# A gate/up kernel stage whose scale sums move along TensorE's products and whose operand buffers change hands product by product

## The chip, the cores and the metric

The kernel runs on one core of a Trainium2 chip. A core has five engines with an instruction stream each: TensorE (PE, with PEld for its weight loads), VectorE (DVE), ScalarE (ACT), GpSimd (POOL) and SyncE (SP), which here issues all DMA transfers. Each engine takes its instructions in the order in which the program has them, and semaphores make it wait for others. The metric is the time of one execution in microseconds (us). Before the change the median of three runs is 2845.04 us (2842.7 to 2848.43).

## The reference, cut to what matters

One layer of an encoder over 2048 tokens of width 1024. The change touches the channel mixer:

```python
h2 = rmsnorm(r, norm2_g[i])
gate = dwconv(h2 @ ffn_wg[i], ffn_conv_w[i], FFN_CONV_LEFT) + ffn_conv_b[i]
r = r + (jax.nn.gelu(gate) * (h2 @ ffn_wu[i])) @ ffn_wd[i]
```

`ffn_wg` and `ffn_wu` are 1024 x 2816, `ffn_wd` 2816 x 1024, the convolution has 3 taps along the tokens. Ahead of it stand the mixers and their output projection, behind it a gated per-layer embedding and a last norm.

## The kernel before, in words

**Arithmetic.** Every float32 operand is split into two float16 parts, high and low, scaled by a power of two, and a product is three float16 products of these parts. On top of it, a product of 2 x 2 blocks is made with seven block products instead of eight (Strassen's scheme in Winograd's form): `PROD` says which of the seven left and which of the seven right operands the products 1 to 7 take, `LEFT` and `RIGHT` say how the operands arise from the four blocks by sums and differences.

**Tiling of the gate/up stage.** The weights come in 22 groups n of 256 output columns, even n for the gate, odd n for the up projection; j = n // 2 counts pairs. The 2048 tokens are two halves u. A unit (n, u) is seven products of 12 matmuls 128x128 by 128x512 (line 1684). `units` (line 1687) puts the products of neighbouring units in turn: product 1 of a unit, then 3 and 7 of the unit before, then 2 and 5, then 4 of the unit before, then 6. So unit (n, 1)'s last product, 4, stands between products 5 and 6 of unit (n+1, 0). A product leaves its result in a bank of PSUM. Its evacuation goes over ACT (line 1859, products 1, 6, 5, 4) or over DVE as an addition (line 1864, products 2, 3, 7).

**Weight groups.** `pair_weights` prepares group n: two loads of 512 KB into two staging buffers (line 1789), the norm's gain on POOL (line 1792), the squares on ACT (line 1795), an add of the two sums on DVE (line 1797), and on PE a matmul with a matrix of ones that sums over the partitions, the scale matmul (line 1800), here called the sum. Six small DVE steps make the power of two from it (lines 382 to 392, `pow2_scale`). Then `operands` makes seven left operands: some need a POOL sum or difference of blocks first (line 1665), each is then split on ACT (line 1640) and DVE (line 1642) into its buffer. The buffers are two sets of seven, for even and odd n. The staging buffers are loaded again when all seven splits of a group are done. Before the change, the splits of group n begin when the last product of unit (n-2, 1) has been put into the program (`pdone`).

**Around it on the same engines.** For each pair j, `gate_tile` does the convolution and gelu of two gate tiles (lines 1906, 1909, 1911, 1913, 1917), `mult` multiplies with the up projection on POOL (line 1927), `act_post` splits the results and writes them out (lines 1945 to 1960), and `row_squares` loads rows of the down weights for their squares (lines 2026, 2028). Behind the stage, the down weights are loaded (line 2064) and split, the embedding's products run (line 438), two further sums stand on PE (line 567 for the embedding's weights, line 2049 for the down weights), and the down products follow.

**What sets the order.** The program is written by a list scheduler, `Sched`. Work is a set of generator streams; each yields a step with the engines and the nanoseconds that it is taken to last (`st`), an event to wait for (`W`) or memory to allocate (`M`). The scheduler keeps a planned time of each engine, and always issues the step with the earliest planned start (`LOOK` weighs a stream's priority against it). `lag` in a step adds to its planned start. An event carries the planned time at which it was fired. All this happens when the program is built; on the chip only the order of each engine's stream and the semaphores are left.

Of the kernel before, what the change touches and what calls it, by code (L numbers as in the profile page):

```python
# [16 lines left out]
S = SEQ = 2048  # L17
# [4 lines left out]
KB = 1024  # L22
# [4 lines left out]
SPOT, LX, LD = 0, 0, 0  # L27
ORDER = "q1 k1 lx1 lg1 lx3 v3 q0 k0 v0 q3 lx0 k3 lg3 k2 lg0 q2 v2 v1 z0 lx2 lg2 z1 z2 ow0 z3 ow1".split()
# [20 lines left out]
class Arena:  # L49
# [9 lines left out]
    def take(self, nbytes, high=False):  # L59
        nbytes = (nbytes + 63) // 64 * 64  # L60
        free = self.lists[nbytes <= 512]

        for page in (PAGE, 64) if nbytes % PAGE == 0 else (64,):
            for o, n in reversed(free) if high else free:
                off = (o + n - nbytes) // page * page if high else -(-o // page) * page
                if o <= off and off + nbytes <= o + n:
                    free.remove((o, n))
                    free += [x for x in ((o, off - o), (off + nbytes, o + n - off - nbytes)) if x[1]]
                    free.sort()
                    return Buf(self, off, nbytes)  # L70
        return None
# [79 lines left out]
class Sched:  # L151
# [43 lines left out]
    def settle(self, s):  # L195
# [11 lines left out]
        if kind == "m":  # L207

            if any(o.spec and o.spec[0] == "m" and o.prio < s.prio and o is not s for o in self.streams):
                return False  # L210
            got = []
            for n in s.spec[1]:
                b = self.A.take(n, s.spec[2])
                if b is None:
                    for x in got:
                        x.free()
                    return False
                got.append(b)
            self.value = got
            return True  # L220
# [63 lines left out]
def W(*name):  # L284
    return ("w", name)
# [52 lines left out]
class Kern:  # L338
# [1330 lines left out]
    def product(self, U, p):  # L1669
# [6 lines left out]
        for i in range(0, m, PER):  # L1676
# [6 lines left out]
            for j, (l, r) in enumerate(part):  # L1683
                self.nc.tensor.matmul(out, l, r, start=(p in (1, 2, 5) and i + j == 0), stop=(p in (2, 3, 4) and i + j == m - 1), skip_group_check=True)  # L1684
        S.spawn(U.evac(p), PR["evac"])
# [84 lines left out]
    def pair_weights(self):  # L1770
# [3 lines left out]
        for n in range(22):  # L1774
# [10 lines left out]
            ops = w.ops = [(b.f16(4, 128), b.f16(4, 128, at=KB)) for b in sets[n % 2]]  # L1785
# [12 lines left out]
            b = yield st(pe=20, bank=1)  # L1798
# [4 lines left out]
            if n > 1:  # L1803
                yield W("pdone", n - 2)
            blocks = [v[i][:, z * 4 : z * 4 + 4] for i in range(2) for z in range(2)]
            put = lambda i, a, w=w: self.split(a, *w.ops[i], 512, w.s)
# [841 lines left out]
```

## Time and profile before

| | |
|---|---|
| median of three runs | 2845.04 us |
| the profiled execution | 2846.02 us, its span 2844.3 us |
| mean granted TensorE clock | 0.961 |
| busy: PE, DVE, ACT, POOL | 90%, 63%, 52%, 34% |
| gate/up stage from behind the sum of group 1 | 1313.3 to 2151.8 us, 838.5 us |
| from there to the down products | 151.2 us |

A row of the timeline gives the start from the span's start, the length, the engine, the line, the operation with the tiles that it writes and reads, shapes, and a count where neighbours are merged; in brackets stands how long the engine was idle before and what released it. `arena` is the one tile in SBUF from which all buffers are cut, `P` a bank of PSUM. Matmuls overlap: the next begins before the modelled end of the one before. [...]

### The profile page before, as it was taken

The page shows a single profiled execution, that of the slowest core. Times are in us where ns is not written, and L with a number is a line of the kernel's source. Part 1 is how long each engine was busy: PE and PEld are TensorE (multiplying, and loading weights), DVE is VectorE, ACT ScalarE, POOL GpSimd, SP SyncE. Part 2 cuts the span into 40 slices and gives each one's busy share as a digit, 9 for nine tenths or more (in the row PEclk, how much of TensorE's full clock was granted, in tenths as well). Part 3 has the DMA queues.
Part 4 walks back from the last instruction along what each step waited for, and adds up shares of the span by engine and source line. Part 5 has one row for each costly group of instructions (what it writes and reads, how often), then busy time and mean ns, then how long its engine had stood idle before and what let it go on. Part 6 is the DMA issues. An engine that isn't in the chain of part 4 may idle for free. (4 is left out here: it accounts for less than half of the span.)

```text
span 2844.3 us, 39697 instructions
## 1 busy us (share of the span) xinstructions
PE 2563.4 (90%) x13918; PEld 1289.5 (45%) x13918; DVE 1797.1 (63%) x3717; ACT 1477.3 (52%) x3042; POOL 977.1 (34%) x686
## 2 busy tenths in 40 slices
PE   5997998889889987976999999999997599999898
PEld 2553454466466653432444444444443244444343
DVE  7668877878784776565566666667768831211358
ACT  6676857764566764254556656666556610101323
POOL 1135335536410022234555656555545600000000
PEclk9998999999999998988999999999999899999999
DMA  9332241475454467396132333323335854556963
GB/s 246 76 96 67 82 123 53 119 208 171 115 160 145 132 214 255 86 212 147 52 93 88 96 108 106 104 87 101 104 97 175 251 182 146 168 168 218 284 176 145
DMA packets 478279, 402.31 MB, mean 141 GB/s; under 512 B 203648, under 2 KB 407296, under 8 KB 478080
## 3 DMA queue, kind: packets, MB, share of 16 engines
q1 hardware_dynamic: 478080, 399.78, 48.2%
q8 instruction: 110, 1.80, 0.3%
q14 instruction: 89, 0.73, 0.1%
HBM read 231.39 MB, written 130.55 MB: 127 GB/s over the span
## 5 line engine op out<-in xcount | busy, mean ns | idle before, releaser
L1684 PE MATMUL P<-arena 128*128 128x512 f16 x5313 | 1163.4, 382 | 2.3 <-DVE arena L2094 1.4
L438 PE MATMUL P<-arena 128*128 128x512 f16 x4032 | 966.8, 389 | 56.3 <-DMA arena<-catl 13.6
L1684 PEld LDWEIGHTS <-arena 128*128 128x128 f16 x5313 | 523.4, 99 | 633.3 <-issue 19.1
L438 PEld LDWEIGHTS <-arena 128*128 128x128 f16 x4032 | 397.8, 101 | 491.2 <-issue 61.4
L1642 DVE SCALAR_TENSOR_TENSOR arena<-arena 128x512 f16<-128x512 f32 (+2 forms) x340 | 416.0, 1257 | 196.3 <-ACT arena L1640 196.1
L1665 POOL TENSOR_TENSOR arena<-arena 128x512 f32<-128x512 f32 (+1 forms) x208 | 367.9, 1770 | 293.9 <-DVE arena L1642 197.7
L1640 ACT ACTIVATE arena<-arena 128x512 f16<-128x512 f32 (+2 forms) x340 | 267.7, 821 | 289.4 <-DMA actd<-arena 65.4
L1927 POOL TENSOR_TENSOR arena<-arena 128x512 f32<-128x512 f32 x88 | 146.4, 1683 | 153.7 <-ACT arena L1917 90.4
L2094 DVE SCALAR_TENSOR_TENSOR arena<-P,arena 128x512 f32<-128x512 f32 x63 | 46.1, 749 | 241.4 <-PE P L1684 221.2
L538 POOL TENSOR_TENSOR arena<-arena 128x1024 f32<-128x1024 f32 (+1 forms) x41 | 82.9, 2027 | 300.6 <-DMA arena<-in_w_in_dram 175.7
L1859 ACT ACTIVATE arena<-P 128x512 f32<-128x512 f32 x176 | 103.5, 588 | 95.4 <-PE P L1684 80.5
L1222 POOL TENSOR_TENSOR arena<-arena 128x512 f32<-128x512 f32 x64 | 119.1, 1876 | 76.0 <-DVE arena L1172 62.2
L699 DVE SCALAR_TENSOR_TENSOR arena<-P,arena 128x511 f32<-128x511 f32 (+1 forms) x192 | 141.8, 742 | 2.0
L2121 ACT ACTIVATE arena<-arena 128x1024 bf16<-128x1024 f32 x16 | 16.9, 1055 | 228.8 <-DVE arena L2094 174.0
L1864 DVE TENSOR_TENSOR arena<-P,arena 128x512 f32<-128x512 f32 x132 | 89.3, 684 | 72.2 <-PE P L1684 68.3
L1792 POOL TENSOR_TENSOR arena<-arena 128x1024 f32<-128x1024 f32 x44 | 92.3, 2107 | 110.4 <-DMA arena<-in_w_gu_dram 51.8
L1419 ACT ACTIVATE arena<-P,arena 128x128 f32<-128x128 f32 x128 | 46.8, 365 | 88.9 <-PE P L1413 69.3
L1424 PE MATMUL P<-arena 128*128 128x128 f32 x256 | 60.3, 318 | 19.5 <-ACT arena L1422 12.8
L862 PE MATMUL P<-arena 128*128 128x512 f32 x128 | 66.3, 634 | 11.7 <-DVE arena L699 5.2
L1430 DVE SCALAR_TENSOR_TENSOR arena<-arena,P 128x128 f32<-128x128 f32 x128 | 43.7, 343 | 52.4 <-PE P L1425 23.4
L1125 POOL TENSOR_TENSOR arena<-arena 128x512 f32<-128x512 f32 x32 | 39.3, 1227 | 108.3 <-DVE arena L1122 90.1
L1274 PE MATMUL P<-arena 32*32 32x32 f32 (+1 forms) x1792 | 63.3, 208 | 13.3 <-issue 6.8
(232 smaller groups left out, 3380.7 us busy)
## 6 DMA issues: line engine op xcount, KB each, us to landing
arena<-hd SPq DMA_DIRECT2D x160, 256.0 KB, 3.1
actd<-arena SPq DMA_DIRECT2D x77, 512.0 KB, 3.7
arena<-actd SPq DMA_DIRECT2D x49, 704.0 KB, 4.1
arena<-in_w_gu_dram SPq DMA_DIRECT2D x44, 512.0 KB, 4.3
arena<-in_x_dram SPq DMA_DIRECT2D x32, 512.0 KB, 6.4
at<-arena SPq DMA_DIRECT2D x64, 256.0 KB, 2.8
arena<-at SPq DMA_DIRECT2D x128, 128.0 KB, 3.0
rd<-arena SPq DMA_DIRECT2D x32, 512.0 KB, 5.2
```

What stands on the lines that cost most here:

```text
L438: self.nc.tensor.matmul(out, l, r, start=(i + j == 0), stop=(i + j == m - 1))
L538: nc.gpsimd.tensor_tensor(at(i), at(i), gain[:, ks[i], None].to_broadcast([128, m, n]), op=ALU.mult)
L699: nc.vector.scalar_tensor_tensor(a[:, lo:hi], P[:, lo - sh : hi - sh], tp[:, j : j + 1], a[:, lo:hi], op0=ALU.mult, op1=ALU.add)
L1222: nc.gpsimd.tensor_tensor(pv[:, i % 2], a(slice(2 * i, 2 * i + 2)), b(slice(2 * i, 2 * i + 2)), op=ALU.mult)
L1640: nc.scalar.activation(hi, x, AF.Copy, scale=scale)
L1642: nc.vector.scalar_tensor_tensor(lo, x, scale, hi, op0=ALU.mult, op1=ALU.subtract)
L1665: nc.gpsimd.tensor_tensor(v[at], v[p], v[q], op=ALU.add if plus else ALU.subtract)
L1684: self.nc.tensor.matmul(out, l, r, start=(p in (1, 2, 5) and i + j == 0), stop=(p in (2, 3, 4) and i + j == m - 1), skip_group_check=True)
L1792: nc.gpsimd.tensor_tensor(v[i], v[i], c["g2"][:, :, None].to_broadcast([128, KT, 128]), op=ALU.mult)
L1859: nc.scalar.activation(d, P, AF.Copy)
L1864: nc.vector.tensor_tensor(d, P, d, op=ALU.add)
L1927: nc.gpsimd.tensor_tensor(v, v, U.buf.f32(2, 2, 4, 128)[:, i, s], op=ALU.mult)
```

## The change

It has three parts. First, the sum of a group gets a planned lag, 5000 ns for the groups from 2 on and 3000 ns for groups 0 and 1. Second, the splits no longer wait for the last product of unit (n-2, 1): each product fires an event "last" when it has been put into the program, the buffers of a set are handed on so that the operand made first gets the buffer whose last product comes first, and each split waits for that product alone. Third, an allocation of several buffers that finds no room on page bounds is tried again without them.

```diff
+AFTER_SUM = 5000
...
-            got = []
-            for n in s.spec[1]:
-                b = self.A.take(n, s.spec[2])
...
+            for pages in (True, False):
+                got = []
+                for n in s.spec[1]:
+                    b = self.A.take(n, s.spec[2], pages)
...
+        S.fire(U.key, "last", p)
         S.spawn(U.evac(p), PR["evac"])
...
-            ops = w.ops = [(b.f16(4, 128), b.f16(4, 128, at=KB)) for b in sets[n % 2]]
+            if n > 1:
+
+                old = [PROD[p][0] for p in (1, 2, 5, 6, 3, 7, 4)]
+                new = [i for i, _, _ in LEFT]
+                frees = {i: next(p for p in PROD if PROD[p][0] == k) for i, k in zip(new, old)}
+                sets[n % 2] = [sets[n % 2][old[new.index(i)]] for i in range(7)]
+            w.ops = [(b.f16(4, 128), b.f16(4, 128, at=KB)) for b in sets[n % 2]]
...
-            b = yield st(pe=20, bank=1)
+            b = yield st(pe=20, bank=1, lag=AFTER_SUM if n > 1 else 3000)
...
-            if n > 1:
-                yield W("pdone", n - 2)
...
-            put = lambda i, a, w=w: self.split(a, *w.ops[i], 512, w.s)
+
+            def put(i, a, n=n, w=w):
+                if n > 1:
+                    yield W(("gu", n - 2, 1), "last", frees[i])
+                yield from self.split(a, *w.ops[i], 512, w.s)
```

The number of instructions of each kind is the same on every engine. In the changed kernel the lines below `take` are numbered up to 13 higher: L1684 is L1687, L1800 is L1810, L1642 is L1645, L1864 is L1877, L1797 is L1807, L1906, L1911 and L1913 are L1919, L1924 and L1926, L382 to L392 are L385 to L395.

PE around the sum of group 2, before (P2_66 is the bank in which product 4 of unit (0, 0) ends; 112 product matmuls of the stage stand ahead of the sum):

```order
L1684 LDWEIGHTS arena_63
L1684 MATMUL P2_66<-arena_63 128x512
L1800 MATMUL P3_67<-arena_63 128x1
L1684 LDWEIGHTS arena_63
L1684 MATMUL P2_66<-arena_63 128x512
```

and now (P6_70 is the bank of products 5 and 3 of unit (0, 1); 148 product matmuls stand ahead):

```order
L1687 LDWEIGHTS arena_63
L1687 MATMUL P6_70<-arena_63 128x512
L1810 MATMUL P5_69<-arena_63 128x1
L1687 LDWEIGHTS arena_63
L1687 MATMUL P6_70<-arena_63 128x512
```

The sum of group 2 moved behind three more products. In the later groups the count of product matmuls ahead of the sum is smaller than before: 300 for 358 in group 3, 1472 for 1488 in group 10, 1650 for 1702 in group 11.

DVE around the add of group 11, before (the banks of the evacuations: P2_66 and P7_71 are products 3 and 7 of unit (9, 0), P0_64 product 2 of unit (9, 1), P6_70, P4_68 and P1_65 products 3 and 7 of unit (9, 1) and 2 of unit (10, 0); the three L1642 are the last splits of group 10):

```order
L1911 SCALAR_TENSOR_TENSOR arena_63<-arena_63 128x2047
L1864 TENSOR_TENSOR arena_63<-P2_66,arena_63 128x512
L1864 TENSOR_TENSOR arena_63<-P7_71,arena_63 128x512
L1913 SCALAR_TENSOR_TENSOR arena_63<-arena_63 128x2047
L1911 SCALAR_TENSOR_TENSOR arena_63<-arena_63 128x2047
L1864 TENSOR_TENSOR arena_63<-P0_64,arena_63 128x512
L1913 SCALAR_TENSOR_TENSOR arena_63<-arena_63 128x2047
L1642 SCALAR_TENSOR_TENSOR arena_63<-arena_63 128x512 x3
L1864 TENSOR_TENSOR arena_63<-P6_70,arena_63 128x512
L1864 TENSOR_TENSOR arena_63<-P4_68,arena_63 128x512
L1864 TENSOR_TENSOR arena_63<-P1_65,arena_63 128x512
L1797 TENSOR_TENSOR arena_63<-arena_63 128x1
```

and now (P7_71 and P6_70 are products 3 and 7 of unit (9, 0), P3_67 product 2 of unit (9, 1); the two L1645 of 128x512 are the last splits of group 10):

```order
L1645 SCALAR_TENSOR_TENSOR arena_63<-arena_63 128x8x128 x2
L1645 SCALAR_TENSOR_TENSOR arena_63<-arena_63 128x512 x2
L1919 TENSOR_SCALAR arena_63<-arena_63 128x3 x2
L1924 SCALAR_TENSOR_TENSOR arena_63<-arena_63 128x2047 x2
L1877 TENSOR_TENSOR arena_63<-P7_71,arena_63 128x512
L1877 TENSOR_TENSOR arena_63<-P6_70,arena_63 128x512
L1926 SCALAR_TENSOR_TENSOR arena_63<-arena_63 128x2047 x2
L1877 TENSOR_TENSOR arena_63<-P3_67,arena_63 128x512
L1807 TENSOR_TENSOR arena_63<-arena_63 128x1
L385 TENSOR_SCALAR arena_63<-P2_66 128x1
```

The last splits of group 10 moved from behind the convolution to ahead of it, the add from behind product 2 of unit (10, 0) to behind product 2 of unit (9, 1). The first step of the scale, L385, stands directly behind the add; the sum that it reads stands on PE three and a half products behind product 2 of unit (9, 1).

## Rows read from the trace of the kernel before

**Rows 1.** The page, part 1 (busy us, share of the span, instructions by engine) and the line of part 2 with the granted TensorE clock in tenths, in 40 slices of 71.1 us.

```profile
PE 2563.4 (90%) x13918; PEld 1289.5 (45%) x13918; DVE 1797.1 (63%) x3717; ACT 1477.3 (52%) x3042; POOL 977.1 (34%) x686
...
PEclk9998999999999998988999999999999899999999
```

**Rows 2.** Busy time by stage, of all instructions: bounds of the stretch in us, its length, then of each engine busy us and instructions, the granted TensorE clock, the share of the DMA engines and GB/s. The second stretch is the gate/up stage from behind the sum of group 1, the third the work between it and the down products.

```profile
0.00:1313.30 1313.30, 1133.90 (x7414) 648.17 (x7415) 944.54 (x2359) 802.23 (x1930) 427.46 (x386) 0.95 0.52 145
1313.30:2151.80 838.50, 805.77 (x3679) 362.31 (x3680) 542.85 (x764) 493.31 (x826) 462.07 (x251) 0.98 0.31 94
2151.80:2303.00 151.20, 104.68 (x436) 44.57 (x436) 113.75 (x109) 83.18 (x126) 87.59 (x51) 0.86 0.69 205
```

**Rows 3.** The chain that ended last, in order of time: start us, us, what.

```profile
2083.56 0.38 PE P L1800 x2
2083.94 48.77 PE P L1684 x218
...
2303.39 328.93 PE P L1684 x1524
```

**Rows 4.** TensorE's waits from 1313.3 to 2151.8 us: who waited for whom, us in total, times, longest us.

```profile
PE P L1800 <- DVE arena L1797: 31.3, 19, 6.2
PE P L1800 <- DVE arena L382: 0.6, 1, 0.6
```

**Rows 5.** TensorE's timeline over the sums of groups 9, 10 and 11: start us, us, engine, line, operation, in brackets the idle time before and its releaser.

```profile
1621.82 26.49 PE L1684 MATMUL P<-arena 128*128 128x512 f16 x122
1648.92 0.38 PE L1800 MATMUL P<-arena 128*128 128x1 f32 x2 [0.61 <-DVE arena L1797]
1649.17 46.35 PE L1684 MATMUL P<-arena 128*128 128x512 f16 x214
1697.43 0.38 PE L1800 MATMUL P<-arena 128*128 128x1 f32 x2 [1.91 <-DVE arena L1797]
1697.67 2.91 PE L1684 MATMUL P<-arena 128*128 128x512 f16 x9
```

**Rows 6.** The same view at the sums of groups 1 and 2.

```profile
1312.91 0.58 PE L1800 MATMUL P<-arena 128*128 128x1 f32 x2 [17.90 <-DVE arena L1797]
...
1335.13 0.58 PE L1800 MATMUL P<-arena 128*128 128x1 f32 x2 [6.24 <-DVE arena L1797]
```

**Rows 7.** Timelines of the other engines at the sum of group 11 (load, gain, square, add, first step of the scale) and, in the last two rows, at that of group 10. SPq is SyncE's queue of DMA issues.

```profile
1687.45 0.81 SPq L1789 DMA_DIRECT2D arena<-in_w_gu_dram  x2
1694.10 1.90 POOL L1792 TENSOR_TENSOR arena<-arena 128x1024 f32<-128x1024 f32 x1
1696.03 1.06 ACT L1795 ACTIVATE arena<-arena 128x1024 bf16<-128x1024 f32 x1 [0.83 <-POOL arena L1792]
1697.21 0.16 DVE L1797 TENSOR_TENSOR arena<-arena 128x1 f32<-128x1 f32 x1 [3.07 <-ACT arena L1795]
1697.85 0.16 DVE L382 TENSOR_SCALAR arena<-P 128x1 f32<-128x1 f32 x1 [0.47 <-PE P L1800]
...
1646.50 4.78 POOL L1665 TENSOR_TENSOR arena<-arena 128x1024 f32<-128x1024 f32 x2 [1.40 <-DVE arena L1642]
1647.69 1.18 DVE L1797 TENSOR_TENSOR arena<-arena 128x1 f32<-128x1 f32 x1 [1.27 <-ACT arena L1795]
```

**Rows 8.** Stretches with a low granted clock (columns as in rows 2): the first and the last of five of 3.4 us behind sums of odd groups (the others begin at 1698.8, 1852.4 and 2006.0), the one at the sum of group 2, and the 7 us behind the sum of group 1.

```profile
1545.20:1548.60 3.40, 3.40 (x10) 1.20 (x9) 0.18 (x2) 0.54 (x3) 0.00 (x0) 0.50 0.25 76
...
2084.50:2087.90 3.40, 3.40 (x10) 1.23 (x9) 1.90 (x11) 1.44 (x4) 0.00 (x0) 0.50 0.01 2
1333.60:1340.40 6.80, 5.27 (x14) 2.21 (x15) 1.10 (x7) 2.23 (x4) 0.10 (x1) 0.50 0.00 0
1313.00:1320.00 7.00, 7.00 (x26) 3.09 (x27) 5.24 (x13) 3.42 (x6) 3.40 (x2) 0.75 0.71 135
```

**Rows 9.** ScalarE's and VectorE's timelines between the sums of groups 10 and 11: the convolution and the last splits of group 10.

```profile
1665.72 0.57 ACT L1859 ACTIVATE arena<-P 128x512 f32<-128x512 f32 x1
1668.40 4.07 ACT L1909 ACTIVATE arena<-arena 128x2048 f32<-128x2048 f32 x2
...
1670.52 2.40 DVE L1911 SCALAR_TENSOR_TENSOR arena<-arena 128x2047 f32<-128x2047 f32 x1 [0.88 <-ACT arena L1909]
1672.84 1.27 DVE L1864 TENSOR_TENSOR arena<-P,arena 128x512 f32<-128x512 f32 x2
1674.04 2.33 DVE L1913 SCALAR_TENSOR_TENSOR arena<-arena 128x2047 f32<-128x2047 f32 x1
1679.16 3.23 DVE L1913 SCALAR_TENSOR_TENSOR arena<-arena 128x2047 f32<-128x2047 f32 x1
1682.32 5.11 DVE L1642 SCALAR_TENSOR_TENSOR arena<-arena 128x512 f16<-128x512 f32 x3
```

**Rows 10.** TensorE's timeline at the end of the stage and behind it, and the longest wait of SyncE's queue from 2133 to 2300 us (us in total, times, longest).

```profile
2142.04 0.28 PE L567 MATMUL P<-arena 128*128 128x1 f32 x2
2151.83 2.75 PE L1684 MATMUL P<-arena 128*128 128x512 f16 x12 [0.86 <-DVE arena L1864]
...
2163.30 0.58 PE L2049 MATMUL P<-arena 128*128 128x1 f32 x2 [2.37 <-DVE arena L2046]
...
SPq L2064 <- DVE arena L1642: 36.8, 8, 8.6
```

More of the change, by code (lines that the diff above doesn't have):

```diff
@@ L57, in __init__, with take @@
         self.lists = [[(0, self.edge)], [(self.edge, SMALL)]]
-    def take(self, nbytes, high=False):
+    def take(self, nbytes, high=False, pages=True):
         nbytes = (nbytes + 63) // 64 * 64
         free = self.lists[nbytes <= 512]
-        for page in (PAGE, 64) if nbytes % PAGE == 0 else (64,):
+        for page in (PAGE, 64) if pages and nbytes % PAGE == 0 else (64,):
             for o, n in reversed(free) if high else free:
@@ L210, in settle @@
                 return False
-            got = []
-            for n in s.spec[1]:
-                b = self.A.take(n, s.spec[2])
[L214 to L220, printed above, removed]
+            for pages in (True, False):
+                got = []
+                for n in s.spec[1]:
+                    b = self.A.take(n, s.spec[2], pages)
+                    if b is None:
+                        for x in got:
+                            x.free()
+                        break
+                    got.append(b)
+                else:
+                    self.value = got
+                    return True
         return False
```

## Prediction

> **What bounds the kernel now.** I read the page's busy times first, then the span cut into stages, then the chain that ended last, then TensorE's own waits in the stage of the change, and last the timelines of single groups. TensorE (PE) is busy for 90% of the span, VectorE (DVE) for 63% [rows 1]. The change sits in the gate/up stage, from the first product of the unit (0,1) at 1313.4 us to the last product at 2151.8 us: 838.5 us, and PE stands on the chain there (48.77 us of products run up to its end without a stop, [rows 2, 3]). So a microsecond that PE loses there is a microsecond of the span.
>
> How much does it lose? A run of 214 product matmuls without a wait takes 46.35 us, of which the last one's modelled length is 0.38: (46.35 - 0.38) / 213 = 0.2158 us a matmul [rows 5]. The stage has 44 units x 7 products x 12 matmuls = 3696, less 48 ahead of 1313.4 and the 12 after 2151.8: 3636 x 0.2158 = 784.6 us. So 838.5 - 784.6 = 53.9 us are lost. TensorE waits there for practically one thing: the scale matmul L1800 for the add L1797 on DVE, 31.3 us in 19 waits [rows 4]. (That view counts from the modelled end of the matmul before, 0.16 us after the next could have started.)
>
> The waits have a pattern. In an odd group (11) PE stands from 1695.5 to 1697.43; the chain behind it is the load L1789 issued at 1687.45, the second product with the gain on POOL at 1694.10, the second square on ACT at 1696.03, the add at 1697.21 [rows 5, 7]. In an even group (10) the wait is 0.61 us: the add, 0.16 us in the odd group, took 1.18 us beside a pair of POOL tensor-tensors, and ended where the first of them does, half of 4.78 us behind 1646.50 [rows 7]. Group 2 waits 6.24 us, group 1 waits 17.90 us [rows 6].
>
> [...]
>
> **The change part by part.**
>
> *The sums.* No instruction is added or removed on any engine; only order and addresses change. In program order the sum of group 2 goes from 112 to 148 product matmuls, so 36 x 0.2158 = 7.8 us later. For the groups from 3 on it goes the other way: group 11 from 1702 matmuls ahead of it to 1650, 11.2 us earlier, group 10 from 1488 to 1472, 3.5 us earlier. "Later" holds only against the add. What makes it possible is the second part.
>
> *The operands.* Before, all 7 splits of group n stand behind the last product of unit (n-2,1). Now each waits for the product that leaves its buffer, six of seven splits go ahead of that point, and the staging buffers come free sooner. Group 11's load waited for group 10's last three splits, which ran at 1682.32 behind the convolution steps L1911 and L1913 and ended as the load was issued at 1687.45 [rows 7, 9]. In the new order those splits stand ahead of L1906, thus ahead of about 1668.4, so the load can go some 19 us earlier. From issue to add it took 1697.21 - 1687.45 = 9.8 us, so the chain alone would allow the add at about 1678.
>
> But the add now stands on DVE behind two L1911, two evacuations, two L1913 and one more evacuation. ACT's two L1909 stand directly behind the evacuation that ended at 1666.3 (in the old times, 1665.72 + 0.57); the first ends at 1668.4. From there two L1911 of 2.4, two evacuations, 1.27, two L1913 of about 2.8 (between 2.33 and 3.23) and an evacuation, 0.64, make 12.3: add at 1680.7, done at 1680.9 [rows 9]. PE gets to the sum 11.2 us before 1695.3, at 1684.1. So about 3 us are to spare in odd groups. In even groups the add has only an evacuation ahead of it, the sum stands 2.67 products (32 matmuls, 6.9 us) behind that product, less about 1 us for the evacuation: some 6 us to spare, which also covers the 1.18 us add.
>
> *The sum of the stage.* Of the 53.9 us these stay: the sum's own passage, 1649.17 - 1648.92 = 0.25 us x 20 = 5.0; the slow clock behind group 1's wait, 1.5 (a granted clock of 0.75 over 7 us is 1.75 lost, 0.25 of it the sum's own); the end of the stage, 0.9 for an evacuation and 0.3 for the sum L567, 1.2 [rows 5, 8, 10]. Left are 46.2 us. Of these the clock is 5 x 3.4 / 2 = 8.5 plus 2.4 (half of 6.8 less the 1.5 us in which PE still waited), and the waits 35.
>
> What comes back: group 2's add ended just ahead of its sum at 1335.1; two more splits of the residual pairs now stand ahead of group 1's scale on DVE (0.64 us each if they last as an evacuation does, [rows 9]), so 1336.4; PE gets there at 1313.4 + 100 x 0.2158 + 1.5 = 1336.5. I charge 1.0 (0 to 3). Rest waits in odd groups: 1.0 over all (bounds 0 and 10 x 2.3 = 23, taken near 0 because of the 3 us to spare). Group 1's wait: the DVE and ACT rows up to its add are the same, so 0 (it could give up to 17.9 if another address freed its buffers).
>
> *What PE could newly wait for.* The evacuation of product 7 now stands behind two L1911. By the same count it ends at 1668.4 + 4.8 + 1.3 = 1674.5; product 4, which needs it, starts 11 products after 1649.17, at 1677.7: 3.2 us of cover, so 0. Behind the scale's first DVE step (it waits for the sum) stand two splits and the next evacuations; the sum is done at 1684.4, the evacuation's own product only at 1688. Also 0.
>
> *Behind the stage.* Two late sums move by a few matmuls: L567 by 4 earlier, L2049 by 6 later; it waited 2.37 us [rows 10]. The loads and splits of the down weights set this stretch (SyncE waits 36.8 us for splits before such loads, [rows 10]), and their number stays. I charge 1.0 (-4 to +5).
>
> Sum: -46 + 1 + 1 + 1 = -43 us on the profiled execution's 2846.0 us: 2803; that run was 1.0 above the median of the runs shown, 2845.0, so **2802 us**.
>
> **The rivals.**
>
> *Odd groups stay late.* The 3 us hang on the convolution steps. If POOL slows DVE more than here (L1913 took 2.33 once and 3.23 once), or ACT brings L1909 some 4 us later, half of an odd wait is left: 10 x 1.1 and the five clock drops, 8.5: 19.5 back, about 2822. For it: the add's new place behind 12.3 us of DVE work. Against: it needs everything at its long value. 0.20.
>
> *The clock drops are not the sums' doing.* Then the waits go and the drops stay: +10.9, 2813. The rows speak against it: every drop starts within 4 us after a wait, and between the waits PE has none. [...] 0.06.
>
> *More than that.* Group 1's wait also shrinks, or the loads behind the stage gain: 10 us better, 2792. For it: addresses change and SyncE's rows behind the stage move. Against: the rows up to group 1's add do not. 0.07.
>
> *Slower: the sum goes up and its chain doesn't.* In odd groups PE reaches the sum 11.2 us earlier and waited 2.3 us already. If the add moves up by x, PE waits 13.5 - x. It is slower than before from x below about 9 us (10 x 4.6 = 46). At x = 5 the waits are 85 us, about 2885. For it: the staging hangs on the last of seven splits, whose buffer comes free no earlier than before. [...] DVE's rows here do run in the order of the program, and so the add cannot pass the convolution. Against: even behind them it stands at 1680.9, x = 16. 0.04.
>
> *Nothing to tell.* Waits of equal size elsewhere, 2845: 0.03.
>
> **How the numbers follow.** Forecast 0.60, with its own range 2796 to 2811; rivals 0.20, 0.06, 0.07, 0.04, 0.03. From 2794 to 2824 some 8 in 10 are held: below lies half of the "more" case, above the slower case, no change and the far part of the late odd groups. About 0.2%, 5.7 us, is what a measurement of this kernel can tell from no change. Faster: 0.60 + 0.20 + 0.06 + 0.07 = 0.93; same 0.03; slower 0.04.
>
> **What would show it.** In the new profile: PE's waits for the add in the stage under 3 us without group 1; the step from one product to the next over a sum about 0.47 us; granted clock 1.00 from group 3 to the end of the stage; the stage at 790 to 797 us; the load L1789 of an odd group issued ahead of the two L1913 rather than behind them; DVE idle for some microseconds at the scale's first step. Wrong it is if PE waits on evacuations (L1859, L1864) in front of products 3 or 4, if the odd sums still wait, or if the stretch from the stage's end to the first long run of down products grows from 151 us by over 5.

## The result: 2816.1 us, some 28 of the 43 us forecast

The changed kernel takes 2816.09 us (median of 4 runs, 2810.7 to 2819.91) against 2843.87 us for the kernel before (4 runs): ratio 0.9899, 95% interval 0.9877 to 0.9921. It is faster by 1.0%, and 14 us above the forecast of 2802. The profiled execution is one of 2819.91 us with a span of 2818.1 us, 26.2 us shorter than the span before.

The page's part 1 and the line with the granted clock:

```profile
PE 2554.9 (91%) x13918; PEld 1291.6 (46%) x13918; DVE 1797.2 (64%) x3717; ACT 1478.3 (52%) x3042; POOL 983.3 (35%) x686
PEclk9998999999999997988999999999998799999999
```

Against [rows 1] PE is busy for 8.5 us less with the same instructions (12.9 less in the stage, where most of the slow clock is gone, 2.7 more on either side of it) and POOL for 6.2 us more with the same 686. Busy time by stage, cut as in [rows 2]: up to the product behind the sum of group 1, the gate/up stage, the transition, the down products (bounds, length, busy us of PE, PEld, DVE, ACT, POOL with instructions, clock, DMA share, GB/s):

```profile
0.00:1315.99 1315.99, 1136.55 (x7414) 650.96 (x7415) 945.99 (x2360) 803.66 (x1930) 424.29 (x386) 0.95 0.51 144
1315.99:2122.20 806.21, 792.86 (x3679) 361.26 (x3680) 542.98 (x766) 493.65 (x826) 472.93 (x251) 1.00 0.33 99
2122.20:2276.60 154.40, 107.40 (x437) 45.31 (x437) 112.62 (x108) 82.23 (x125) 86.08 (x50) 0.85 0.63 194
```

The stage went from 838.5 to 806.2 us (-32.3). Ahead of it 2.7 us were lost (1313.3 to 1315.99), and the transition behind it grew from 151.2 to 154.4. TensorE's waits from 1300 to 2180 us, in place of [rows 4] (us in total, times, longest; the L441 and L2062 rows lie behind the stage):

```profile
PE P L1810 <- DVE arena L1807: 17.3, 1, 17.3
PE P L1687 <- ACT arena L1872: 10.8, 8, 2.8
...
PE P L1687 <- DVE arena L1877: 2.4, 1, 2.4
```

The 17.3 us are group 1's sum, which waited 17.90 before [rows 6]. Of the 31.3 us that the sums of groups 2 to 21 waited, nothing is left. In their place products now wait for evacuations. Taken from start to start against the 0.2158 us of a matmul, the products lose 15.0 us: nine waits of 0.27 to 2.99 us, 12.4 us in all, eight of them at product 6 of an odd group's second unit (with 80, 108, 136, ... 276 products of the stage ahead of it), one at the product 4 just before, and 2.6 at the stage's last product. The timelines around the sum of group 11, whose counterparts are in [rows 5, 7, 9], show where such a wait comes from:

```profile
1650.88 1.52 SPq L1799 DMA_DIRECT2D arena<-in_w_gu_dram  x2
1653.15 4.61 DVE L1924 SCALAR_TENSOR_TENSOR arena<-arena 128x2047 f32<-128x2047 f32 x2 [2.03 <-ACT arena L1922]
1655.69 7.73 POOL L1802 TENSOR_TENSOR arena<-arena 128x1024 f32<-128x1024 f32 x2 [7.25 <-DMA arena<-in_w_gu_dram]
1658.88 6.68 DVE L1926 SCALAR_TENSOR_TENSOR arena<-arena 128x2047 f32<-128x2047 f32 x2
1663.45 1.06 ACT L1805 ACTIVATE arena<-arena 128x1024 bf16<-128x1024 f32 x1 [2.75 <-POOL arena L1802]
1664.42 0.19 ACT L1805 ACTIVATION_READ_ACCUMULATOR arena<-arena 128x1 f32 x1
1664.51 0.58 ACT L1872 ACTIVATE arena<-P 128x512 f32<-128x512 f32 x1
1665.14 4.04 PE L1687 MATMUL P<-arena 128*128 128x512 f16 x18 [1.09 <-ACT arena L1872]
1666.09 0.14 DVE L1807 TENSOR_TENSOR arena<-arena 128x1 f32<-128x1 f32 x1
1669.02 0.28 PE L1810 MATMUL P<-arena 128*128 128x1 f32 x2
1669.34 0.16 DVE L385 TENSOR_SCALAR arena<-P 128x1 f32<-128x1 f32 x1 [3.10 <-PE P L1810]
```

Read it downwards. The load is issued 18.1 us ahead of the sum (10.0 before), the add is done at 1666.23, 2.8 us ahead of the sum, and PE passes the sum without a stop. So far this is the forecast. But the early load brings the two gains on POOL beside convolution steps on DVE, the second L1924 and both L1926. The gains take 3.87 us in the mean (1.90 in [rows 7]), and the two L1926 take 6.68 together, one by one 2.79 and 3.98 (2.33 at best in [rows 9]). ACT stands 2.75 us at the second square L1805 until the gain is done, and behind that square in ACT's stream is the evacuation L1872 of product 1, for which product 6 waits on PE.

One clock drop is left in the stage behind group 1's, at the longest of these waits (2.99 us, PE goes on at 1962.86). A second one of 3.4 us begins at 2122.5, at the wait of 2.6 us before the last product, and makes that product, which counts to the transition, 1.7 us longer. The first:

```profile
1962.10:1965.50 3.40, 2.64 (x7) 0.99 (x7) 2.70 (x9) 3.40 (x6) 0.81 (x1) 0.50 0.02 5
```

### The profile page after: what moved, and what is told of

Same layout as the page of the kernel before. It is cut to its first block, busy times and chain, and to the rows that moved or that the text cites. A ratio compares the mean times of both kernels' runs of the same rounds, so it can differ in the third digit from the quotient of the medians.

```text
span 2818.1 us, 39755 instructions
## 1 busy us (share of the span) xinstructions
PE 2554.9 (91%) x13918; PEld 1291.6 (46%) x13918; DVE 1797.2 (64%) x3717; ACT 1478.3 (52%) x3042; POOL 983.3 (35%) x686
## 4 chain that ended last, share of the span: by engine, by line
PE 42%; DVE 9%; POOL 5%; ACT 4%; DMA 4%; issue 3%; SPq 1%; DVEq 0%; ACTq 0%; POOLq 0%
PE P L1687 29%; PE P L441 11%; DVE arena L1645 4%; POOL arena L1668 3%; POOL arena L1802 2%; DMA arena<-arena 2%; PE P L2179 1%; ACT arena L1643 1%; DMA arena<-in_w_gu_dram 1%; SPq L2353 1%; PE P L1427 1%; ACT arena L1872 0%; DVE arena L1924 0%; DVE arena L1641 0%; ACT arena L1639 0%
## 5 line engine op out<-in xcount | busy, mean ns | idle before, releaser
L1687 PE MATMUL P<-arena 128*128 128x512 f16 x5313 | 1157.3, 380 | 14.8 <-ACT arena L1872 10.8
L441 PE MATMUL P<-arena 128*128 128x512 f16 x4032 | 967.0, 389 | 56.8 <-DMA arena<-catl 18.5
L1687 PEld LDWEIGHTS <-arena 128*128 128x128 f16 x5313 | 521.4, 98 | 642.1 <-issue 25.0
L441 PEld LDWEIGHTS <-arena 128*128 128x128 f16 x4032 | 397.9, 101 | 491.1 <-issue 60.3
L1645 DVE SCALAR_TENSOR_TENSOR arena<-arena 128x512 f16<-128x512 f32 (+2 forms) x340 | 422.9, 1274 | 176.6 <-ACT arena L1643 175.5
L1668 POOL TENSOR_TENSOR arena<-arena 128x512 f32<-128x512 f32 (+1 forms) x208 | 375.5, 1813 | 275.7 <-DVE arena L1645 183.2
L1802 POOL TENSOR_TENSOR arena<-arena 128x1024 f32<-128x1024 f32 x44 | 116.3, 2662 | 133.8 <-DMA arena<-in_w_gu_dram 111.5
L1940 POOL TENSOR_TENSOR arena<-arena 128x512 f32<-128x512 f32 x88 | 123.1, 1419 | 105.5 <-ACT arena L1930 61.9
L1225 POOL TENSOR_TENSOR arena<-arena 128x512 f32<-128x512 f32 x64 | 118.3, 1865 | 79.9 <-DVE arena L1175 60.4
L1872 ACT ACTIVATE arena<-P 128x512 f32<-128x512 f32 x176 | 102.9, 587 | 61.6 <-PE P L1687 60.2
L1877 DVE TENSOR_TENSOR arena<-P,arena 128x512 f32<-128x512 f32 x132 | 88.8, 681 | 14.7 <-PE P L1687 14.6
L2179 PE MATMUL P<-arena 128*128 128x512 f16 x231 | 53.6, 396 | 29.7 <-DMA arena<-actd 29.7
L1128 POOL TENSOR_TENSOR arena<-arena 128x512 f32<-128x512 f32 x32 | 39.3, 1227 | 109.0 <-DVE arena L1125 91.7
```

Source lines behind the costliest of these rows:

```text
L441: self.nc.tensor.matmul(out, l, r, start=(i + j == 0), stop=(i + j == m - 1))
L1225: nc.gpsimd.tensor_tensor(pv[:, i % 2], a(slice(2 * i, 2 * i + 2)), b(slice(2 * i, 2 * i + 2)), op=ALU.mult)
L1645: nc.vector.scalar_tensor_tensor(lo, x, scale, hi, op0=ALU.mult, op1=ALU.subtract)
L1668: nc.gpsimd.tensor_tensor(v[at], v[p], v[q], op=ALU.add if plus else ALU.subtract)
L1802: nc.gpsimd.tensor_tensor(v[i], v[i], c["g2"][:, :, None].to_broadcast([128, KT, 128]), op=ALU.mult)
L1872: nc.scalar.activation(d, P, AF.Copy)
```

## The experiments

Theory A: what PE still loses it loses at product 6, because the second square of an odd group, waiting for a slow gain, stands ahead of an evacuation on ACT; and the lag of groups 0 and 1 costs the 3 us ahead of the stage. The rivals stand in the expectations. The medians of the kernel before, beside these runs, lie between 2841.7 and 2843.9 us.

**1. The lag alone.** The sums get their lag; the splits wait for the last product as before.

```diff
-            b = yield st(pe=20, bank=1)
+            b = yield st(pe=20, bank=1, lag=5000 if n > 1 else 3000)
```

> Only the lag of the sums (5000 ns for the groups from 2 on, 3000 ns for groups 0 and 1); the splits still wait for the last product of unit (n-2, 1), and no buffers change hands. The sums then stand 2 to 5.5 products later than before the change (group 11 behind 143.8 products for 141.8, group 10 behind 129.5 for 124.0), and a group has 7 products, some 18 us, from its sum to its first use. Theory A (the later place against the add is what pays, the takeover only makes room for it): the waits for the add are gone (31 us before, below 3 now) and the clock drops with them, and 7 products are enough for the splits: the stage is 40 to 47 us shorter than before the change, the time near 2803, better than with the whole change. Rival B (the takeover is needed, since the splits come too late for the first products): TensorE waits for splits (L1642) in front of product 1, 2 or 5 of each unit (n, 0), 2 us or more for each group, and the time is 2820 to 2850.

Measured: 2843.96 us, ratio 1.001 (1.000 to 1.002). The sums lose nothing, the products 34.0 us, and there are seven clock drops of 3.4 us (stage 835.3). TensorE's waits in the stage, and a stretch at group 10 (lines numbered as before the change):

```profile
PE P L1684 <- ACT arena L1859: 23.9, 12, 2.7
PE P L1684 <- DVE arena L1864: 6.5, 10, 2.1
```

```profile
1668.09 1.32 ACT L1640 ACTIVATE arena<-arena 128x512 f16<-128x512 f32 x2
1669.94 0.72 ACT L1640 ACTIVATE arena<-arena 128x512 f16<-128x512 f32 x1 [0.54 <-POOL arena L1665]
1673.21 0.72 ACT L1640 ACTIVATE arena<-arena 128x512 f16<-128x512 f32 x1 [2.55 <-POOL arena L1665]
1674.24 1.06 ACT L1859 ACTIVATE arena<-P 128x512 f32<-128x512 f32 x2
1674.87 1.44 PE L1684 MATMUL P<-arena 128*128 128x512 f16 x3 [2.68 <-ACT arena L1859]
```

Here splits that wait for POOL's sums and differences stand ahead of the evacuation. Theory A as put for this run fell. Rival B has the time (2820 to 2850) but not the mechanism: no product waits for a split itself, all 22 waits are for evacuations. Moving the sum alone does not remove the loss, it moves it to the products, 23.6 of the 34.0 us to product 6; at group 10 a split rather than a square is in the way.

**2. The takeover alone.** The whole change, without the lag.

```diff
-            b = yield st(pe=20, bank=1, lag=AFTER_SUM if n > 1 else 3000)
+            b = yield st(pe=20, bank=1)
```

> The whole change without any lag: buffers are handed on product by product, the sums stand 1.3 to 3 products earlier than with the lag (group 11 behind 136.2 products for 137.5, group 10 behind 120.7 for 122.7, group 2 behind 9.3 for 12.3). Theory A: the spare time at the sums measured in the changed kernel (2.8 us in odd groups) is used up in odd groups and nearly so in even ones, group 2 waits 6 us again as before the change: waits for the add of 8 to 25 us in all, some clock drops come back. On ScalarE the second square of an odd group stands behind the evacuation of product 1 here, so if the square in front of that evacuation is what makes product 6 wait in the changed kernel, those waits (10.8 us) are gone here. Time 2808 to 2825. Rival B (the lag is what pays): the waits for the add are as long as before the change, 30 us, and the time is 2835 or more.

Measured: 2875.8 us, ratio 1.012 (1.0105 to 1.0135): slower than before. The sums lose 50.8 us, and ten clock drops of 3.4 or 6.8 us follow those of group 2 and of the odd groups from 5 on. The sum of group 9:

```profile
1603.24 5.80 POOL L1802 TENSOR_TENSOR arena<-arena 128x1024 f32<-128x1024 f32 x2 [10.21 <-DMA arena<-in_w_gu_dram]
1603.38 3.90 DVE L1926 SCALAR_TENSOR_TENSOR arena<-arena 128x2047 f32<-128x2047 f32 x1
1614.38 1.22 DVE L1807 TENSOR_TENSOR arena<-arena 128x1 f32<-128x1 f32 x1
1615.66 0.58 PE L1810 MATMUL P<-arena 128*128 128x1 f32 x2 [4.54 <-DVE arena L1807]
```

The takeover moves the sum up in PE's order (108.17 products ahead of it), and the add behind the convolution cannot follow. That is the mechanism of the forecast's slower rival, in a kernel without the lag. With both parts the sum of group 9 stands at 109.5, and its wait is gone. Product 6 itself loses nothing here, as expected where the square stands behind the evacuation; but PE is held at the sums beside it, so this alone proves little.

**3. The square behind the evacuation.** In the changed kernel the second square of odd groups is planned 3 us later, the sum's place in the plan kept (137.83 products ahead of group 11's, 137.5 in the changed kernel).

```diff
-                yield st(act=c_act(1024))
+                yield st(act=c_act(1024), lag=3000 if n > 1 and n % 2 and i else 0)
...
-            b = yield st(pe=20, bank=1, lag=AFTER_SUM if n > 1 else 3000)
+            b = yield st(pe=20, bank=1, lag=AFTER_SUM - (3000 if n % 2 else 0) if n > 1 else 3000)
```

> The changed kernel with one row moved on ScalarE: in odd groups the second square (L1795 of the kernel before) is planned 3000 ns later and comes to stand behind the evacuation of product 1 of unit (n, 1) instead of ahead of it; the sum keeps its place to a third of a product. Theory A (the evacuation of product 1 stood in ScalarE's queue behind a square that waited for a slow gain on GpSimd, and product 6 waited for that evacuation): TensorE's waits in front of product 6 (10.8 us, 8 of them) fall below 2 us, the clock drop at 1962 goes, the stage is 11 to 14 us shorter, the time 12 to 14 us below the changed kernel, near 2803. Rival B (the evacuation waits for the convolution on VectorE, whose first half is done later because two L1911 now run before the first L1913): the waits stay at 1.2 to 3 us a group, and the time stays within 3 us of the changed kernel. Rival C (it helps there but the sum, now nearer to its add, waits instead): the waits for the add come back with 1 us or more a group, time 2808 to 2818.

Measured: 2819.65 us, ratio 0.9921 (0.991 to 0.9933), stage 807.0. The products' losses fall from 15.0 to 3.2 us, and those of the sums rise to 12.3 (0.7 to 2.2 us in each odd group):

```profile
PE P L1810 <- DVE arena L1807: 10.0, 9, 1.9
PE P L1687 <- DVE arena L1877: 1.8, 2, 1.4
PE P L1687 <- ACT arena L1872: 0.6, 1, 0.6
```

So the square does hold the evacuation, as theory A has it, and rival C is right as well: a square put later holds the add instead, unless the sum moves too. One clock drop of 3.4 us is left, at one of these sums.

**4. No early lag.** The changed kernel, groups 0 and 1 without lag.

```diff
-            b = yield st(pe=20, bank=1, lag=AFTER_SUM if n > 1 else 3000)
+            b = yield st(pe=20, bank=1, lag=AFTER_SUM if n > 1 else 0)
```

> The changed kernel without the 3000 ns lag for groups 0 and 1. The sum of group 0 goes back to its old place among the output projection's products, and two splits of the residual pairs go back behind the first step of group 1's scale. Theory A (the 3 us that the changed kernel lost ahead of the stage come from this lag): the first gate/up product starts 2 to 3 us earlier, and the time is 2 to 3 us lower. Rival B (that part differs from execution to execution): no difference that can be told from the changed kernel, and the first product starts anywhere between 1284 and 1288.

Measured: 2812.76 us, ratio 0.9902 (0.9888 to 0.9916). The stage is the same (806.4): its products lose 13.7 us, and group 2's sum, which stands behind 11.17 products instead of 12.33, now waits 1.5 us (1.3 and 1.5 in experiments 7 and 9). The first gate/up product starts at 1283.65 us instead of 1287.69. That start is theory A's; by ratio the two kernels can't be told apart.

**5 to 7, with the changed kernel once more beside them.** Run again, the changed kernel takes 2815.96 us (0.9904; stage 804.8, transition 151.3); its products lose 12.4 us at the same places, and the clock falls at the same product 248.

> The changed kernel once more, as it is, so that the three beside it can be set against it on one chip. All theories: 2816 us, 0.990 of the kernel before; in its trace the products of the gate/up stage lose about 15 us, nearly all at product 6 of the units of odd groups, and the sums nothing.

Experiment 5 keeps the later square and lets the sum keep its 5 us behind it (139.0 products ahead of group 11's sum):

```diff
-                yield st(act=c_act(1024))
+                yield st(act=c_act(1024), lag=3000 if n > 1 and n % 2 and i else 0)
```

> The changed kernel, with the second square of each odd group planned 3 us later, so that on ScalarE it stands behind the evacuation that product 6 needs; and the sum keeps its 5 us behind that square, so that it comes 1.2 products (some 3 us) later than in the run in which only the square moved. Theory A (PE loses at product 6 because the square that waits for the gain stands ahead of product 1's evacuation, and the sum needs as much room behind the square as it had): the waits at product 6 fall from 15.0 us to about 3, and the 12.3 us that the sums lost with the square alone moved are gone too; the stage takes 806.2 - 12.0 - 1.7 (its one clock drop) = some 793 us, and the kernel 2803 us, 0.986 of the kernel before. Rival C (one of the two waits is always there, as the gain is what is late): sums and product 6 together still lose 10 to 15 us, 2814 to 2819 us. Rival D (a later sum makes the splits late): the wait moves to the first product that reads the odd group's operands, 2815 us or more.

Measured: 2812.24 us (0.9893, 0.9878 to 0.9908), stage 802.7. Up to product 219 of the stage's 308 neither sums nor products of odd groups lose anything (the changed kernel loses 1.2 us at product 6 in each of five odd groups there); 0.97 us at product 9 is new. Group 7, in which the square (1518.56) now stands behind three evacuations and PE runs through:

```profile
1504.83 17.43 PE L1687 MATMUL P<-arena 128*128 128x512 f16 x80
1518.08 0.58 ACT L1872 ACTIVATE arena<-P 128x512 f32<-128x512 f32 x1
1518.56 1.05 ACT L1805 ACTIVATE arena<-arena 128x1024 bf16<-128x1024 f32 x1
1519.73 0.16 DVE L1807 TENSOR_TENSOR arena<-arena 128x1 f32<-128x1 f32 x1 [2.90 <-ACT arena L1805]
1522.09 0.28 PE L1810 MATMUL P<-arena 128*128 128x1 f32 x2
```

From product 219 on thirteen waits (0.25 to 1.59 us) and 1.5 at the last product make 11.1 us. Theory A holds for the first 219 products. Its 2803 us did not come: of the 13 us that it promised the stage gave 2 to 3.5 (against 804.8 and 806.2), as its last part waits elsewhere.

Experiment 6 plans the gains at twice their length (sums at 131.67 and 146.0 products for groups 10 and 11):

```diff
-                yield st(pool=c_pool(1024) * 0.8)
+                yield st(pool=c_pool(1024) * 1.6)
```

> The changed kernel, with each of GpSimd's gains put into the plan at twice its length, which moves gains, squares and sums of all groups: an odd group's sum stands some 8.5 products later, its two gains stand further apart in GpSimd's order, and its squares behind the evacuations of products 1 and 5. Theory A with the gain as the late step (a gain that runs beside VectorE's convolution takes 3.9 us where one alone takes 1.9): the mean gain falls from 2.66 to about 2.1 us, product 6 and the sums lose under 4 us together, 2803 to 2806 us. Rival E (what counts is not the gain but how much stands ahead of an evacuation on ScalarE's queue): other work, the convolution's own, now stands ahead of product 1's evacuation, product 6 or 3 loses as much as before, 2812 to 2820 us.

Measured: 2885.81 us (1.0151, 1.0131 to 1.017), the slowest of all; the products lose 53.7 us. Group 17, the longest but one of its waits:

```profile
1929.33 2.33 ACT L1643 ACTIVATE arena<-arena 128x512 f16<-128x512 f32 x4
1932.18 4.60 DVE L1926 SCALAR_TENSOR_TENSOR arena<-arena 128x2047 f32<-128x2047 f32 x2
1934.62 1.08 ACT L1872 ACTIVATE arena<-P 128x512 f32<-128x512 f32 x2 [2.95 <-DVE arena L1926]
1935.27 3.14 PE L1687 MATMUL P<-arena 128*128 128x512 f16 x7 [8.54 <-ACT arena L1872]
```

The L1926 run at their short length here (2.30 us each), the stage's gains take 2.07 us in the mean (2.73 in the changed kernel), and PE waits all the same: the evacuations stand behind splits and behind a wait for the convolution. So theory A with the gain as the late step fails for this kernel, and rival E has the mechanism, what stands ahead of the evacuation; but its 2812 to 2820 us were far too low.

Experiment 7 is experiment 5 without the early lag.

```diff
-            b = yield st(pe=20, bank=1, lag=AFTER_SUM if n > 1 else 3000)
+            b = yield st(pe=20, bank=1, lag=AFTER_SUM if n > 1 else 0)
```

> The kernel with the later square and sum of the odd groups, and no wait put ahead of the sums of groups 0 and 1. Theory A: the 3.2 us by which the first gate/up product came later (1284.5 to 1287.7) come back on top of the 13 of the later square: 2800 us, 0.985 of the kernel before, and 16 below the changed kernel. Rival C: only those 3 us, 2812 to 2814 us. Rival D: 2812 us or more, with the wait at the first product on the odd group's operands.

Measured: 2809.39 us (2808.04 to 2810.62 in 4 runs; 0.9885, 0.9868 to 0.9901). Its runs lie below all four of the changed kernel beside it (2812.47 to 2816.74): 6.6 us faster, the lowest median here, though not the 2800 of theory A. Its first gate/up product starts at 1281.6, its stage takes 802.4.

**8. The odd groups' gain on VectorE** (in the groups from 3 on; the plan puts it behind the convolution).

```diff
-                yield st(pool=c_pool(1024) * 0.8)
-                nc.gpsimd.tensor_tensor(v[i], v[i], c["g2"][:, :, None].to_broadcast([128, KT, 128]), op=ALU.mult)
+                on_dve = n > 1 and n % 2
+                yield st(dve=1200) if on_dve else st(pool=c_pool(1024) * 0.8)
+                (nc.vector if on_dve else nc.gpsimd).tensor_tensor(v[i], v[i], c["g2"][:, :, None].to_broadcast([128, KT, 128]), op=ALU.mult)
```

> The changed kernel, with the two gains of each odd group from 3 on made by VectorE instead of GpSimd; the plan puts them behind the convolution and product 2's evacuation, the two squares behind product 4's evacuation, and the sum two products later. Theory A with the shared cause (gain and convolution slow each other where they run side by side): the odd groups' L1926 steps fall from 3.3 us to the 2.34 that they take alone, the gains take some 1.3 us each (twice the 0.68 of a 128x512 operation on this engine), and product 6 loses under 1 us a group in the first half of the stage: 2806 to 2811 us, 0.987 to 0.9885 of the kernel before. Rival F (the wait moves to VectorE's queue: the add waits there for the squares, and the evacuation of product 3 stands behind it): the products lose 1 us or more in each odd group behind that add, 2815 us or more. Rival G (the steps are no quicker apart: the 3.3 us is not GpSimd's doing): L1926 stays at 3.3 us.

Measured: 2812.38 us (0.9895, 0.9879 to 0.9912), stage 801.9. Groups of instructions from 1480 to 1860 us (busy, mean ns of one, idle before), first of the changed kernel, then of this one, whose lines from the gain on count one higher:

```profile
L1802 POOL TENSOR_TENSOR arena<-arena 128x1024 f32<-128x1024 f32 x20 | 57.6, 2900 | 57.0 <-DMA arena<-in_w_gu_dram 50.0 <-DVE arena L1924 7.1
L1926 DVE SCALAR_TENSOR_TENSOR arena<-arena 128x2047 f32<-128x2047 f32 x10 | 33.4, 3382 | 0.0
```

```profile
L1927 DVE SCALAR_TENSOR_TENSOR arena<-arena 128x2047 f32<-128x2047 f32 x10 | 23.0, 2343 | 0.0
L1803 DVE TENSOR_TENSOR arena<-arena 128x1024 f32<-128x1024 f32 x10 | 21.8, 2217 | 0.0
L1803 POOL TENSOR_TENSOR arena<-arena 128x1024 f32<-128x1024 f32 x10 | 18.8, 1896 | 21.0 <-DMA arena<-in_w_gu_dram 21.0
```

With the odd gains off POOL the convolution's L1926 is back at 2343 ns from 3382. The even groups' gains take 1896 ns; the 2900 above is the mean of these and of the 3.87 us of the odd ones. So it was POOL's gain that stretched L1926 here, and rival G is out. On DVE the gain takes 2.2 us, not the 1.3 expected; from group 5 on all of these gains run beside POOL's multiplications (L1941). Up to product 219 the products lose 0.24 us (against 6.2 in the changed kernel's first profile), so rival F is out there. Behind it they lose 11.9. Two waits of 1.37 us among these (products 251 and 279) do go back to the gain's new place, by another way than F's: an evacuation on ACT stands behind the second square, the square behind a split of the embedding's operands (`p_pairs`), the split waits 1.5 us for a scale step on DVE, and that step stands behind the gain. The first gate/up product starts late, at 1290.2, so the median, just above the 2806 to 2811 expected, does not show the stage's gain in full.

**9. Half of it.** Experiment 7, with the later square only in groups 3 to 15.

```diff
-                yield st(act=c_act(1024), lag=3000 if n > 1 and n % 2 and i else 0)
+                yield st(act=c_act(1024), lag=3000 if 1 < n < 16 and n % 2 and i else 0)
```

> The kernel with no wait put ahead of the sums of groups 0 and 1, and the second square of the odd groups planned 3 us later only in groups 3 to 15; from 17 on the order is the changed kernel's. Theory A in the first half alone (product 6 loses nothing there, and what is lost behind product 219 depends on the order there, not on what the first half gains): the products lose some 8 us behind product 219 as in the changed kernel and next to nothing ahead of it, against 11 in the kernel with all odd groups late: 2805 to 2808 us, 0.987 of the kernel before. Rival H (behind product 219 other engines set the pace, and time won ahead of it is lost there): 2810 us or more, with product waits of over 11 us behind product 219.

Measured: 2809.88 us (2806.27 to 2817.48; 0.9892, 0.9873 to 0.9911), not told apart from experiment 7. The waits behind product 219 are the changed kernel's again, 8.0 us (0.56, 0.81, 2.93, 2.02, 1.68), with its clock drop; stage 801.6. So the loss there goes with the order there, not with what the first part gained: 8.0 us against 8.8 and 6.3 in the changed kernel's two profiles, not the over 11 of rival H. But the median is above theory A's 2805 to 2808, and the stage as a whole comes out as in experiment 7, 801.6 against 802.4.

What sets the pace behind product 219 is settled only in part. The traces show that the convolution comes later there against PE. In the changed kernel its first L1924 of each pair starts with 47.9, 75.9, 103.9, 131.9, 159.9 and 187.9 products of the stage begun, 28 apart, and then with 216.2, 244.6 and 272.2, thus 0.3 to 0.7 products late. A product takes 2.59 us, so the 0.7 are 1.8 us, and by about that much the wait of 2.99 us at product 248 is longer than the 1.25 of the first five (3.01 in the second profile of this kernel, 2.99 and 2.93 in experiments 4 and 9, with the same 244.6). With 0.3 the waits are not alike: 0.81 and 2.09 us at products 220 and 276, 0.81 at both in the second profile. In experiments 5 and 7 the last two starts are at 245.4 and 273.4.

What delays the convolution was not tested. Beside it in time stand those operands of the embedding (a load, a square on ACT, six small steps on DVE and a split for each of 16 tiles), which begin at product 212 in the changed kernel and in each of its variants but experiment 6 (191). In experiment 8 the two waits of 1.37 us lead back to them in part, and the longest (2.96 us at product 240) to one of their squares, which stands on ACT for 2.91 us until its load is there. Against this as the whole cause speaks the kernel before: DVE is busier there too, for 54.4 of 72 us against 47.1 in the first part (from 1927 and from 1495 us), but its convolution is not late (216.3, 244.2 and 272.2 after 188.2):

```profile
1495.00:1567.00 72.00, 69.71 (x317) 31.41 (x318) 47.12 (x60) 42.41 (x76) 40.75 (x23) 0.98 0.30 92
1927.00:1999.00 72.00, 69.42 (x323) 31.47 (x323) 54.44 (x88) 44.33 (x68) 41.43 (x23) 1.00 0.31 94
```

## Why the prediction was right, and where it fell short

The mechanism of the main gain was right, the size was not: 28 of 43 us came. The time lies 5 us above the forecast's own range (2796 to 2811). It lies inside 2794 to 2824 because that range also took in the late odd groups (2822), a rival that did not happen; so that the wide range held the time is in part luck. Of the signs named beforehand two failed: the stage takes 806.2 us instead of 790 to 797, and the clock is not at 1.00 to its end. PE's waits on evacuations, named as a sign of being wrong for products 3 and 4, came at product 6.

- **The sums' waits (35 us):** right. They are gone, the odd add is done 2.8 us ahead of its sum (about 3 forecast), the load is issued ahead of the L1926, DVE waits 3.10 us at L385. Group 2 and the odd rests, charged 1.0 each, cost nothing. Experiments 1 and 2 add what the forecast did not say: neither half of the change gains anything alone.
- **The clock (10.9 us):** right in kind. With the waits, six slow stretches at a granted clock of 0.50 went (five of 3.4 us and the one of 6.8 at group 2's sum, [rows 8]), and one of 3.4 us came at a new wait (1.7 back); a further one lies just behind the stage, at its last product. The rival that held the drops to be no doing of the waits is out: in every run here each fall within the stage follows a PE wait, the shortest of 2.1 us (as at group 7 before the change, where PE goes on at 1543.88 and the clock falls at 1545.2), or (experiment 6) two that make 2.8 or more together.
- **The sums' passage,** charged 0.25 us x 20, is 0.15: 2.1 us better.
- **"What PE could newly wait for: ... 0":** this is the step that failed. I looked there at DVE's queue and product 4, and had cover. ACT's queue I did not look at: there the second square moved ahead of an evacuation that product 6 needs. It cost 12.4 us; the end of the stage, charged 0.9, cost 2.6. That the early load would put the gain beside the convolution also followed from [rows 7, 9]: load, gain and L1913 were all there. I weighed the longer L1913 (3.23 us, with POOL's L1927 beside it from 1678.98 on, and 2.33 without, [rows 9]) for the add alone, not for the gain.
- **The stage, summed:** 794.3 forecast (784.6 + 5.0 + 1.5 + 1.2 + 1.0 + 1.0); less 2.1 and 2.0, plus 12.4, 1.7 and the clock's 1.7, makes 806.0; measured 806.2.
- **Ahead of the stage** I saw no cost of the lag of groups 0 and 1. Six profiles with it start the first gate/up product at 1285.8 to 1290.2 us (a seventh, experiment 6, at 1282.75), the five without it, the kernel before among them, at 1281.6 to 1284.6. The medians of experiments 4 and 7 lie 3 us below those of the same kernels with the lag, within the runs' spread. It points to some 3 us, and is not shown.
- **The transition,** charged 1.0, grew by 3.2 in one profile, 1.7 of it the slow clock over the stage's last product, and by 0.1 in the second, which has no such drop: no cost of its own can be told.
- **The rivals:** "odd groups stay late" (2822) is wrong as a mechanism, though part of what it foresaw, L1913 longer beside POOL, is what happened (as L1926 3.38 us in the mean from 1480 to 1860 us, 2.34 in experiment 8 with the odd gains off POOL). The slower rival was wrong for the change, and its mechanism is that of the takeover without the lag (1.012).

## What to carry to other kernels

When a step is moved earlier, follow its whole chain on the queue of every engine that it crosses, and ask what is queued behind each link that can wait: here a square that waits 2.75 us for its input holds an evacuation, and so TensorE. A plan that prices each step alone misses what they cost side by side: at group 11 of the changed kernel the gains on GpSimd took 3.83 and 3.94 us for 1.90, the L1926 on VectorE 2.79 and 3.98 for 2.34. And two halves of a change can each be worth nothing or less (ratios of 1.001 and 1.012 here), and 1% together.

## What the runs showed of the hardware that I had not expected

- A gain, a 128x1024 float32 tensor-tensor on POOL, took 1.90 us with 0.05 us of DVE work beside it and 1.90 with 0.5 us of an evacuation from PSUM (group 11 before the change, at 1694.10 and 1691.02). Beside DVE's 128x2047 steps the two gains of group 11 in the changed kernel took 3.83 and 3.94. The steps themselves took 2.34 (L1924, begun ahead of the first gain), 2.79 and 3.98 (L1926; 2.34 in experiment 8): the pair of gains was longer by 3.9 us, the pair of L1926 by 2.0.
- At group 11 the two engines' steps end in turn: the first gain 1.75 us behind that L1924, the first L1926 2.15 behind the first gain, the second gain 1.75 behind that L1926, the second L1926 2.15 behind the second gain. These steps are near 1.90 and 2.34, the lengths of a gain and an L1926 above. What makes them end so no run shows.
- On DVE the gain took 2.2 us beside POOL's multiplications (experiment 8). What it takes alone there no run shows.
- The clock did not fall at every wait of a kind: it fell at waits of 2.99 (changed kernel) and 2.93 us (experiment 9), at one of three of 2.2 us (experiment 3), at five of nine of 2.1 to 2.7 us (the odd groups from 5 on before the change), and not at one of 2.96 us (experiment 8, no drop in its stage).
